# Quarter buffers for the weights of two experts, and a seventh buffer in the ring

## The chip, the core and the metric

The kernel runs on one core of a Trainium2 chip. The metric is the device time of one launch in microseconds (us); the numbers are fp32 throughout. TensorE (PE) does the matrix products, VectorE (DVE), ScalarE (ACT) and GpSimd (POOL) the rest, and SyncE (SP) issues the transfers (DMAs) that bring weights from the device's memory (HBM) into the core's on-chip memory of 128 partitions.

## The reference, cut to what matters

Two blocks of two layers each run over 256 tokens of width 1024. The first block is where the change lies: a gated linear recurrence and a mixture of experts, then a short convolution and a second mixture of experts. The second block is an S5 state space layer, a squared-ReLU MLP, latent attention and another MLP. A mixture of experts looks like this:

```python
def hierarchical_moe(h, w_group, b_group, w_expert, b_expert, w_gate, w_up, w_down):
    ...                                   # 4 groups of 8 experts, each token goes to 2 of 32
    def expert_block(args):
        xb, e = args
        hb = jax.nn.silu(xb @ w_gate[e]) * (xb @ w_up[e])     # 1024 -> 512
        return hb @ w_down[e]                                 # 512 -> 1024
    ...                                   # gated sum back into the tokens
```

An expert has three matrices of 2 MiB (gate, up, down). The kernel reads all 32 experts, so a mixture moves 192 MiB of weights.

## The kernel before, in words

`moe` (L771) handles the experts in eight groups of four; `e0` is the first expert of a group. A group's four experts are computed side by side: each has 32 token slots, and its products fill a band of 32 rows of PE's output. For one group the order of the program is: `load(e0)` asks for the weights (24 MiB), PE does the gate and up products (L963), ACT the SiLU (L971), DVE the product with up (L972), PE transposes (L977) and does the down products (L1002), ACT and DVE scale them into y (L1005, L1006), and PE adds y back to the tokens (L1014; DVE's addition is L1025). On every second group PE also gathers the tokens for the next two (L911, L912).

Weights come in through `fetch` (recorded as L447): it takes the next buffer of a ring and has SP issue a DMA of 1 MiB into it, 8 KB in each of the 128 partitions. SP waits, in order, until the last reader of the buffer's old contents is done; a buffer that isn't free stops every later load too. One buffer holds a half of one expert's matrix: four of its eight rows per partition (gate, up), one run of 8 KB. The loads of a group are gate half 0 of four experts, up half 0, gate half 1, up half 1, then eight for down. PE takes a block of 16 matmuls for gate or up in one half, four rows times four experts, in which the expert changes fastest. So a block needs four buffers, and all four are in use to its end.

The ring is long in layer two's mixture at first, 17 buffers, and is cut while group e0 = 8 runs: the generator `stages` (L1962), which the mixture advances at set points, calls `shrink` after 12 steps, and from then on the ring is the six buffers of the main pool. The space goes to `s5_prepare`, S5's tables, which the generator then works off in steps between the mixture's own instructions (E and cf on DVE, L1346 `pr`, L1380 and L1416 transposes on PE). A buffer more is added by `grow(1)` in `s5` (L1573) when S5's scan is over. The next loads after the mixture's own are S5's weights. A scheduler orders each engine's instructions by priority and dependence, so that a change of the loads also moves other instructions.

S5's scan keeps working arrays `ro0`, `ro1` and `hc` of 2 KB per partition each in a pool of its own.

Of the kernel before, what the change touches and what calls it, by code (L numbers as in the profile page):

```python
# [8 lines left out]
F32 = mybir.dt.float32  # L9
# [31 lines left out]
KV = 1  # L41
WARMB = 3
G3 = 5
EARLY = 1, 0
N0 = 4
FAST = (0, 1), (0, 1)
# [26 lines left out]
class Net:  # L73
# [697 lines left out]
    def moe(self, layer, rows, stages=()):  # L771


        nc, I, tc = self.nc, self.I, self.tc
# [7 lines left out]
        with ExitStack() as ph:  # L782
# [56 lines left out]
            def logits(n):  # L839
                v.tensor_tensor(lg[:, n, :], self.logits(layer, self.xt[n]), self.br[layer], op=OP.add)  # L840

            if EARLY[N == 3]:
                logits(0)
# [4 lines left out]
            for n in range(2):  # L848
                src = h[n].rearrange("t (p k) -> t k p", k=KD)
                self.pin(a.copy)(xh[n], src)  # L850
                nc.gpsimd.tensor_tensor(xl[n], src, xh[n].bitcast(F32), op=OP.subtract)
            if not EARLY[N == 3]:
                logits(0)
# [8 lines left out]
            for n in range(2):  # L862
                p = self.bank()
# [18 lines left out]
            def load(e):  # L882

                def half(w, hf):
                    out = []
                    for i in range(4):
                        src = w[layer, e + i].rearrange("(p k) f -> p k f", p=128)
                        k = src.shape[1] // 2
                        out.append(self.fetch(src[:, hf * k:hf * k + k, :], [128, k, src.shape[2]]))
                    return out  # L890

                gu = [[half(I[nm], hf) for nm in ("moe_w_gate", "moe_w_up")] for hf in range(2)]
                if e < 28:
                    return gu, [half(I["moe_w_down"], hf) for hf in range(2)]

                src = [I["moe_w_down"][layer, e + i].rearrange("(p k) f -> p k f", p=128) for i in range(4)]
                down = [[self.fetch(x[:, :, 0:512], [128, 4, 512]) for x in src], [self.fetch(None, [128, 4, 512]) for x in src]]
                for c in lasts[1:]:
                    for t, x in zip(down[1], src):
                        self.pin(nc.sync.dma_start)(t[:, :, c.start - 512:c.stop - 512], x[:, :, c])  # L900
                return gu, down
# [22 lines left out]
            def places(e0):  # L924
# [7 lines left out]
                return P  # L932

            first = load(0)
            P = places(0)
            xg_tile = lambda: B.tile([128, 4, 256], F32, name="xg", bufs=2)
            xg = [gather(xg_tile(), P, 256, 0)]
# [11 lines left out]
            for qd in range(8):  # L949

                e0, c0 = 4 * qd, 128 * (qd % 2)
                if qd % 2 == 0 and qd:
                    P, xg = places(e0), []
                wgu, wd = load(e0) if qd else first
                gu = [self.bank() for _ in range(2)]
                for hf in range(2):
                    if len(xg) == hf:
                        xg.append(gather(xg_tile(), P, 256, hf))
                    for m in range(2):
                        for k in range(4):  # L960
                            for i in range(4):
                                c = slice(c0 + 32 * i, c0 + 32 * i + 32)
                                nc.tensor.matmul(gu[m][i * 32:(i + 1) * 32, :], lhsT=xg[hf][:, k, c], rhs=wgu[hf][m][i][:, k, :],  # L963
                                                 start=hf == 0 and k == 0, stop=hf == 1 and k == 3)
                    if qd < 7:
                        next(stages, None)
                if N == 3 and qd == 0:
# [5 lines left out]
                if qd < 7:  # L973
                    next(stages, None)
                p = self.bank("tp")
# [6 lines left out]
                p = self.bank("tp")  # L982
# [15 lines left out]
                def down(c, j, w):  # L998

                    o = ob[c.start // 512][:, c.start % 512:(c.stop - 1) % 512 + 1]  # L1000
                    for e in range(4):
                        nc.tensor.matmul(o[e * 32:(e + 1) * 32, :], lhsT=ht[:, j, e * 32:(e + 1) * 32], rhs=w[e], start=j == 0, stop=j == 3)  # L1002
                    if j == 3:
                        yh, yl = (t[:, c.start % 512:(c.stop - 1) % 512 + 1] for t in y[c.start // 512])
                        a.activation(yh, o, AF.Copy, scale=gs)  # L1005
                        v.scalar_tensor_tensor(yl, o, gs, yh.bitcast(F32), op0=OP.mult, op1=OP.subtract)  # L1006
                        if N == 3 and qd < 7:
                            v.scalar_tensor_tensor(yo[:, c], o, gs, yo[:, c], op0=OP.mult, op1=OP.add)
# [8 lines left out]
                if qd < 7:  # L1017
                    for j in range(4):
                        for c in HALVES:
                            down(c, j, [wd[j // 2][e][:, j % 2, c] for e in range(4)])  # L1020
                        if j % 2:
                            next(stages, None)
                    for n in range(2):
                        for c in HALVES:
                            v.tensor_tensor(h[n][:, c], h[n][:, c], back(n, c), op=OP.add)  # L1025
                    next(stages, None)
                    continue
# [437 lines left out]
    def s5(self):  # L1465
        nc, I, h = self.nc, self.I, self.h
        v, a = nc.vector, nc.scalar
        BL, CL, KT, rho = self.BL, self.CL, self.KT, self.rho
        with ExitStack() as ph:
# [4 lines left out]
            keep = es.enter_context(self.pool("s5k"))  # L1474
# [9 lines left out]
            for q4 in range(4):  # L1484
                p = self.bank()
                for j in range(4):
                    for i, x in enumerate((xh, xl)):
                        nc.tensor.matmul(p, lhsT=self.place[:, 128 * q4 + 3 - j:128 * q4 + 131 - j], rhs=x[:, :, j:SEQ:4],  # L1488
                                         start=j + i == 0, stop=j + i == 4)
# [6 lines left out]
            B = es.enter_context(self.pool("s5b", 2))  # L1496

            ros, hcs = [], []
            for i in range(2):
                ros.append(keep.tile([128, 8, 64], F32, name=f"ro{i}"))  # L1500
                nc.gpsimd.memset(ros[i][:, :, 0:1], 0.0)
            for i in range(4):
                hcs.append([keep.tile([128, 8, 64], F32, name=f"hc{i}{n}") for n in range(2)])
                for n in range(2):
                    nc.gpsimd.memset(hcs[i][n][:, :, 0:1], 0.0)
            v8 = lambda ap: ap.rearrange("p (g n) -> p g n", g=8)
# [36 lines left out]
            for Q in range(4):  # L1543
                py = self.bank()
                for n in range(3):
                    for q in range(8):
                        for y in range(2):
# [5 lines left out]
                            else:  # L1553
                                l, r = hcs[(2 * Q + y) % 4][1][:, q, :], CS[:, g, :]
                            nc.tensor.matmul(py[y * 64:(y + 1) * 64, q * 64:(q + 1) * 64], lhsT=l, rhs=r,
                                             start=n + q == 0, stop=n == 2 and q == 7, skip_group_check=True)
# [6 lines left out]
                p = self.bank("tp")  # L1563
                for i in range(4):
                    nc.tensor.transpose(p[:, i * 128:(i + 1) * 128], yg[:, i].rearrange("p q c -> p (q c)"), self.ident)
                src = p.rearrange("p (i g n) -> p g i n", i=4, g=2)
                for g in range(2):
                    k = 2 * Q + g
# [1 line left out]
            es.close()  # L1570
            self.kept.close()
            self.wide = [(self.right.enter_context(self.pool(f"wide{n}", n, "right")), n) for n in (2, 3)]
            self.grow(1)  # L1573
            self.widen()
            self.F.append(self.ctx.enter_context(self.pool("fb")))
            S = ph.enter_context(self.pool("glus"))
# [375 lines left out]
    def stages0(self):  # L1952
# [4 lines left out]
        self.shrink()  # L1957
        self.grow(G3)
        self.wide_s = ExitStack()
        self.wide = self.wide_s.enter_context(self.pool("wide0", 3, "right"))  # L1960

    def stages(self):  # L1962

        for _ in range(NY):
            yield
        self.shrink()
        self.tables_now = False
        for _ in range(N0):
            yield
        yield from self.s5_prepare()  # L1970

    def run(self):
# [6 lines left out]
        self.wide_s.close()  # L1979
        self.grow(11 - G3)  # L1980
        self.moe(1, [128, 128], self.stages())
# [40 lines left out]
```

## Time and profile before

| what | value |
|---|---|
| median of 3 runs | 1988.52 us (1983.27 to 1994.42) |
| the profiled execution's own time | 1989.83 us |
| its span | 1988.1 us |
| mean granted TensorE clock | 0.906 of full speed |
| PE busy | 1630.0 us, 82% |
| DVE, ACT, POOL busy | 863.1, 508.0, 242.7 us |
| DMA queue of SP | 532.04 MB, 70.7% of 16 engines' span |
| gate/up matmuls, L963 | 410.5 us busy, 187.5 us idle before them |
| down matmuls, L1002 | 220.2 us busy, 17.7 us idle before them |

The span is the profiled execution from its first to its last instruction. A row of instructions gives what line, engine and operation it is, output and inputs by the program's names, and how many; "idle before" is the time in which the engine stood still just ahead of such instructions, with the one it waited for. A window row gives the busy time of each engine in a stretch of the span, the clock that TensorE was granted there as a share of its full speed, the share of time in which the 16 DMA engines were busy, and the traffic. The two rows of matmuls in the table take in both mixtures.

### The profile page before, as it was taken

To read this page: it belongs to the slowest core of one execution; us is meant where nothing else is said; L and a number is where in the kernel's file an instruction comes from. 1 tells how busy PE (TensorE), PEld (TensorE's weight loads), DVE (VectorE), ACT (ScalarE), POOL (GpSimd) and SP (SyncE) were. 2 spreads that over 40 slices of the span, in tenths; PEclk is the share of its full clock that TensorE was granted. 3 is DMA by queue.
4 is the path that set the end of the run, shared out by engine and by line. 5 is a ranking of instruction groups with operands and counts; after the bars stand their busy time and mean duration, and the time that the engine had idled before them with its cause. 6 is when DMAs were issued, how large, how long until landed. Compare 5 with 4: busy or idle time off the path is not lost.

```text
span 1988.1 us, 24934 instructions
## 1 busy us (share of the span) xinstructions
PE 1630.0 (82%) x10043; PEld 1014.4 (51%) x10044; DVE 863.1 (43%) x1724; ACT 508.0 (26%) x811; POOL 242.7 (12%) x263
## 2 busy tenths in 40 slices
PE   7878777777777978766768778678989998898997
PEld 6753211222126953212313222136979997878997
DVE  6872101111008661105313131176776556776555
ACT  4621000000004431000100100022545443564442
POOL 3330000000003230000000000015431003303000
PEclk9889989999898989987878879779899998999999
DMA  9358999999999657998786788884635542425540
GB/s 308 115 212 344 419 420 420 420 419 420 419 402 329 215 191 319 420 420 321 303 340 241 304 336 338 317 187 110 234 127 184 182 160 90 170 85 179 184 147 22
DMA packets 133113, 535.57 MB, mean 269 GB/s; under 512 B 23141, under 2 KB 35686, under 8 KB 85882
## 3 DMA queue, kind: packets, MB, share of 16 engines
q1 hardware_dynamic: 130818, 532.04, 70.7%
q0 software_dynamic: 1856, 1.75, 0.4%
q8 instruction: 81, 1.33, 0.3%
q14 instruction: 46, 0.38, 0.1%
q10 hardware_dynamic: 312, 0.07, 0.0%
HBM read 526.49 MB, written 1.05 MB: 265 GB/s over the span
## 4 chain that ended last, share of the span: by engine, by line
PE 37%; DMA 13%; DVE 7%; ACT 1%; issue 1%; POOL 1%; SPq 0%; DVEq 0%; POOLq 0%; ACTq 0%
DMA raw<-in_moe_w_gate 7%; PE mm L963 5%; PE mm L493 5%; PE mm L491 5%; PE mm L492 5%; DMA raw<-in_moe_w_up 4%; PE tp L492 3%; PE tp L493 3%; PE mm L1002 3%; PE tp L491 3%; DMA raw<-in_moe_w_down 2%; PE tp L1416 1%; DVE wlo L294 1%; PE mm L1488 1%; PE mm L1014 0%
## 5 line engine op out<-in xcount | busy, mean ns | idle before, releaser
L963 PE MATMUL mm<-raw,xg 128*32 128x512 f32 x2048 | 410.5, 738 | 187.5 <-DMA raw<-in_moe_w_up 113.7
L294 DVE TENSOR_TENSOR wlo<-raw,whi 128x1024 fp32r<-128x1024 f32 (+3 forms) x265 | 294.2, 1126 | 185.2 <-ACT whi L293 184.2
L963 PEld LDWEIGHTS mm<-raw,xg 128*32 128x32 f32 x2048 | 86.7, 130 | 494.9 <-DMA raw<-in_moe_w_up 193.5
L293 ACT CAST whi<-raw 128x1024 fp32r<-128x1024 f32 (+3 forms) x265 | 239.0, 917 | 252.7 <-PE mm L493 105.7
L972 DVE TENSOR_TENSOR hh<-hh,mm 128x512 f32<-128x512 f32 x16 | 11.0, 687 | 520.1 <-PE mm L963 520.1
L1002 PE MATMUL mm<-raw,ht 128*32 128x512 f32 (+2 forms) x1120 | 220.2, 612 | 17.7 <-DMA raw<-in_moe_w_down 14.2
L492 PE MATMUL tp<-f,whi 128*128 128x256 f32 x512 | 147.6, 288 | 11.5 <-DVE f L409 11.5
L493 PE MATMUL mm<-whi,f 128*128 128x512 f32 (+3 forms) x432 | 150.2, 348 | 2.1 <-DVE f L409 2.1
L491 PE MATMUL mm<-whi,f 128*128 128x512 f32 (+3 forms) x432 | 151.4, 350 | 0.0
L492 PE MATMUL mm<-wlo,f 128*128 128x512 f32 (+3 forms) x432 | 150.9, 349 | 0.0
L493 PE MATMUL tp<-f,wlo 128*128 128x256 f32 x512 | 146.9, 287 | 0.0
L491 PE MATMUL tp<-f,whi 128*128 128x256 f32 x512 | 146.6, 287 | 0.4 <-ACT f L403 0.2
L1002 PEld LDWEIGHTS mm<-raw,ht 128*32 128x32 f32 x1120 | 54.3, 118 | 142.9 <-issue 97.8
L971 ACT ACTIVATE hh<-mm 128x512 f32<-128x512 f32 x16 | 9.6, 597 | 430.3 <-PE mm L963 430.3
L492 PEld LDWEIGHTS tp<-f,whi 128*128 128x128 f32 x512 | 100.4, 196 | 12.0 <-POOL h L95 11.8
L491 PEld LDWEIGHTS tp<-f,whi 128*128 128x128 f32 x512 | 99.9, 196 | 1.2 <-ACT f L403 0.8
L493 PEld LDWEIGHTS tp<-f,wlo 128*128 128x128 f32 x512 | 100.5, 196 | 0.0
L492 PE MATMUL mm<-xl,whi 128*128 128x272 f32 (+2 forms) x320 | 93.9, 294 | 7.5 <-DVE xl L409 7.1
L491 PE MATMUL mm<-xh,whi 128*128 128x272 f32 (+2 forms) x320 | 93.1, 295 | 0.6 <-ACT yg L663 0.4
L493 PE MATMUL mm<-xh,wlo 128*128 128x272 f32 (+2 forms) x320 | 92.5, 290 | 0.0
L493 PEld LDWEIGHTS mm<-whi,f 128*128 128x128 f32 x432 | 82.3, 190 | 12.7 <-DVE f L409 2.7
L491 PEld LDWEIGHTS mm<-whi,f 128*128 128x128 f32 x432 | 82.6, 191 | 10.3
(609 smaller groups left out, 2504.9 us busy)
## 6 DMA issues: line engine op xcount, KB each, us to landing
raw<-in_moe_w_gate SPq DMA_DIRECT2D x128, 1024.0 KB, 10.3
raw<-in_moe_w_up SPq DMA_DIRECT2D x128, 1024.0 KB, 19.9
raw<-in_moe_w_down SPq DMA_DIRECT2D x120, 1024.0 KB, 16.8
raw<-in_w_ff SPq DMA_DIRECT2D x64, 1024.0 KB, 4.9
raw<-in_sc_w_in SPq DMA_DIRECT2D x12, 1024.0 KB, 12.4
raw<-in_lru_w_in SPq DMA_DIRECT2D x8, 1024.0 KB, 14.0
raw<-in_ssm_w_glu SPq DMA_DIRECT2D x8, 1024.0 KB, 10.7
raw<-in_moe_w_down SPq DMA_DIRECT2D x12, 512.0 KB, 13.3
```

The costliest lines, as they stand in the source:

```text
L293: f(self.nc.scalar.copy)(hi, src)
L294: f(self.nc.vector.tensor_tensor)(lo, src, hi.bitcast(F32), op=OP.subtract)
L491: mm(out, lhsT=lh, rhs=rh, start=first, stop=False, skip_group_check=shared)
L492: mm(out, lhsT=lh, rhs=rl, start=False, stop=False, skip_group_check=shared)
L493: mm(out, lhsT=ll, rhs=rh, start=False, stop=last, skip_group_check=shared)
L963: nc.tensor.matmul(gu[m][i * 32:(i + 1) * 32, :], lhsT=xg[hf][:, k, c], rhs=wgu[hf][m][i][:, k, :], start=hf == 0 and k == 0, stop=hf == 1 ...
L971: a.activation(hh, gu[0], AF.Silu)
L972: v.tensor_tensor(hh, hh, gu[1], op=OP.mult)
L1002: nc.tensor.matmul(o[e * 32:(e + 1) * 32, :], lhsT=ht[:, j, e * 32:(e + 1) * 32], rhs=w[e], start=j == 0, stop=j == 3)
L1416: nc.tensor.matmul(po[:, :, j:4, :], lhsT=sel[:, 67 - 64 * g - j:195 - 64 * g - j], rhs=Kg[:, g, :, 0:4 - j, :], start=n == 0, stop=n == 7)
L1488: nc.tensor.matmul(p, lhsT=self.place[:, 128 * q4 + 3 - j:128 * q4 + 131 - j], rhs=x[:, :, j:SEQ:4], start=j + i == 0, stop=j + i == 4)
```

## The change

A constant FINE = 8 selects layer two's groups from e0 = 8 on. There `load` no longer fills a buffer with half a matrix of one expert but with a quarter of two: two of eight rows for gate and up (one of four for down) of the experts i and i + 1, each in a run of 4 KB per partition, the two experts' matrices lying 2 MiB apart in HBM. Gate and up alternate by quarters, so loads come in pairs. The matmuls of a half are cut into parts of two rows accordingly, 8 matmuls for gate, 8 for up. Down loads in the groups up to e0 = 24 are quarters too; the last group's keep their shape. Directly behind `shrink` a `grow(1)` makes the ring seven buffers long, and the one in `s5` is gone. S5's scan takes `ro0`, `ro1` and the two arrays `hc` of index 0 from one ring buffer.

```diff
@@ -41,6 +41,7 @@
 KV = 1
 WARMB = 3
 G3 = 5
+FINE = 8
 EARLY = 1, 0
 N0 = 4
 FAST = (0, 1), (0, 1)
@@ -889,9 +890,23 @@
                         out.append(self.fetch(src[:, hf * k:hf * k + k, :], [128, k, src.shape[2]]))
                     return out
 
-                gu = [[half(I[nm], hf) for nm in ("moe_w_gate", "moe_w_up")] for hf in range(2)]
+                def quarter(w, kq):
+
+                    out = []
+                    for i in (0, 2):
+                        src = w[layer, e + i:e + i + 2].rearrange("e (p k) f -> p e k f", p=128)
+                        k = src.shape[2] // 4
+                        t = self.fetch(src[:, :, kq * k:kq * k + k, :], [128, 2, k, src.shape[3]])
+                        out += [t[:, 0], t[:, 1]]
+                    return out
+
+                fine = layer == 1 and e >= FINE
+                if fine:
+                    gu = [[quarter(I[nm], kq) for nm in ("moe_w_gate", "moe_w_up")] for kq in range(4)]
+                else:
+                    gu = [[half(I[nm], hf) for nm in ("moe_w_gate", "moe_w_up")] for hf in range(2)]
                 if e < 28:
-                    return gu, [half(I["moe_w_down"], hf) for hf in range(2)]
+                    return gu, [quarter(I["moe_w_down"], j) for j in range(4)] if fine else [half(I["moe_w_down"], hf) for hf in range(2)]
 
                 src = [I["moe_w_down"][layer, e + i].rearrange("(p k) f -> p k f", p=128) for i in range(4)]
                 down = [[self.fetch(x[:, :, 0:512], [128, 4, 512]) for x in src], [self.fetch(None, [128, 4, 512]) for x in src]]
@@ -956,12 +971,15 @@
                 for hf in range(2):
                     if len(xg) == hf:
                         xg.append(gather(xg_tile(), P, 256, hf))
-                    for m in range(2):
-                        for k in range(4):
-                            for i in range(4):
-                                c = slice(c0 + 32 * i, c0 + 32 * i + 32)
-                                nc.tensor.matmul(gu[m][i * 32:(i + 1) * 32, :], lhsT=xg[hf][:, k, c], rhs=wgu[hf][m][i][:, k, :],
-                                                 start=hf == 0 and k == 0, stop=hf == 1 and k == 3)
+
+                    n = len(wgu) // 2
+                    for part in range(n):
+                        for m in range(2):
+                            for k in range(4 // n * part, 4 // n * (part + 1)):
+                                for i in range(4):
+                                    c = slice(c0 + 32 * i, c0 + 32 * i + 32)
+                                    nc.tensor.matmul(gu[m][i * 32:(i + 1) * 32, :], lhsT=xg[hf][:, k, c], rhs=wgu[hf * n + part][m][i][:, k % (4 // n), :],
+                                                     start=hf == 0 and k == 0, stop=hf == 1 and k == 3)
                     if qd < 7:
                         next(stages, None)
                 if N == 3 and qd == 0:
@@ -1017,7 +1035,8 @@
                 if qd < 7:
                     for j in range(4):
                         for c in HALVES:
-                            down(c, j, [wd[j // 2][e][:, j % 2, c] for e in range(4)])
+                            k = 4 // len(wd)
+                            down(c, j, [wd[j // k][e][:, j % k, c] for e in range(4)])
                         if j % 2:
                             next(stages, None)
                     for n in range(2):
@@ -1496,11 +1515,12 @@
             B = es.enter_context(self.pool("s5b", 2))
 
             ros, hcs = [], []
+            t = self.fetch(None, [128, 4, 8, 64])
             for i in range(2):
-                ros.append(keep.tile([128, 8, 64], F32, name=f"ro{i}"))
+                ros.append(t[:, i])
                 nc.gpsimd.memset(ros[i][:, :, 0:1], 0.0)
             for i in range(4):
-                hcs.append([keep.tile([128, 8, 64], F32, name=f"hc{i}{n}") for n in range(2)])
+                hcs.append([keep.tile([128, 8, 64], F32, name=f"hc{i}{n}") if i else t[:, 2 + n] for n in range(2)])
                 for n in range(2):
                     nc.gpsimd.memset(hcs[i][n][:, :, 0:1], 0.0)
             v8 = lambda ap: ap.rearrange("p (g n) -> p g n", g=8)
@@ -1570,7 +1590,6 @@
             es.close()
             self.kept.close()
             self.wide = [(self.right.enter_context(self.pool(f"wide{n}", n, "right")), n) for n in (2, 3)]
-            self.grow(1)
             self.widen()
             self.F.append(self.ctx.enter_context(self.pool("fb")))
             S = ph.enter_context(self.pool("glus"))
@@ -1964,6 +1983,7 @@
         for _ in range(NY):
             yield
         self.shrink()
+        self.grow(1)
         self.tables_now = False
         for _ in range(N0):
             yield
```

On SP the loads of group e0 = 12 read before:

```order
L447 DMA raw<-in_moe_w_gate 128x2048 x4
L447 DMA raw<-in_moe_w_up 128x2048 x4
L447 DMA raw<-in_moe_w_gate 128x2048 x4
L447 DMA raw<-in_moe_w_up 128x2048 x4
L447 DMA raw<-in_moe_w_down 128x2048 x8
```

and now (the line of `fetch` is L448 there):

```order
L448 DMA raw<-in_moe_w_gate 128x2x1024 x2
L448 DMA raw<-in_moe_w_up 128x2x1024 x2
L448 DMA raw<-in_moe_w_gate 128x2x1024 x2
L448 DMA raw<-in_moe_w_up 128x2x1024 x2
L448 DMA raw<-in_moe_w_gate 128x2x1024 x2
L448 DMA raw<-in_moe_w_up 128x2x1024 x2
L448 DMA raw<-in_moe_w_gate 128x2x1024 x2
L448 DMA raw<-in_moe_w_up 128x2x1024 x2
L448 DMA raw<-in_moe_w_down 128x2x1024 x8
```

The count is the same, 16 and 8; gate and up change after every pair instead of every fourth load.

On PE the beginning of the down products of group e0 = 12 reads before as follows (`ht` is the transposed hidden activation, W a table of S5, xh and xl the tokens that are gathered for the next groups):

```order
L1002 MATMUL mm<-raw,ht 32x512 x4
L1380 MATMUL tp<-ident,W 128x128 x8
L911 MATMUL tp<-P_7283,xh_5360 128x256
L912 MATMUL tp<-P_7283,xl_5362 128x256
L911 MATMUL tp<-P_7285,xh_5361 128x256
L912 MATMUL tp<-P_7285,xl_5363 128x256
```

and now, in lines L1020, L1399, L926 and L927:

```order
L1399 MATMUL tp<-ident,W 128x128 x2
L1020 MATMUL mm<-raw,ht 32x512 x4
L1399 MATMUL tp<-ident,W 128x128 x6
L926 MATMUL tp<-P_7286,xh_5360 128x256
L927 MATMUL tp<-P_7286,xl_5362 128x256
L926 MATMUL tp<-P_7288,xh_5361 128x256
L927 MATMUL tp<-P_7288,xl_5363 128x256
L1020 MATMUL mm<-raw,ht 32x512 x4
```

The down products stand in fours, with one gather's four matmuls between the first and the second four; before, fifteen gather matmuls stood there.

On DVE the scaling y of group e0 = 8 and the exponential of S5's preparation (E, mg) read before:

```order
L1201 SCALAR_TENSOR_TENSOR E<-E 128x64
L1006 SCALAR_TENSOR_TENSOR y_6807<-mm,gs,y_6806 128x512
L261 SCALAR_TENSOR_TENSOR E<-E 128x64
L1238 CAST place<-ident 128x128
L1006 SCALAR_TENSOR_TENSOR y_6809<-mm,gs,y_6808 128x512
```

and now, where y is L1024:

```order
L262 SCALAR_TENSOR_TENSOR E<-E 128x64 x3
L263 TENSOR_SCALAR E<-E 128x64
L265 TENSOR_TENSOR mg<-E 128x64
L1298 TENSOR_TENSOR p_7034<-mg,w_6906 128x64
L1024 SCALAR_TENSOR_TENSOR y_6810<-mm,gs,y_6809 128x512
L1024 SCALAR_TENSOR_TENSOR y_6812<-mm,gs,y_6811 128x512
```

The rest of the exponential, up to the first product with mg, has moved ahead of y.

## Rows read from the trace of the kernel before

**Rows 1.** The page, part 2: GB/s that the DMA engines moved, in 40 slices.

```profile
...
GB/s 308 115 212 344 419 420 420 420 419 420 419 402 329 215 191 319 420 420 321 303 340 241 304 336 338 317 187 110 234 127 184 182 160 90 170 85 179 184 147 22
...
```

**Rows 2.** Windows of layer two's MoE; columns: us, busy, PEclk, DMA share, GB/s.

```profile
912.60:957.00 44.40, 29.53 (x129) 6.01 (x128) 17.53 (x72) 1.76 (x4) 0.00 (x0) 0.73 0.83 323
957.00:994.90 37.90, 30.60 (x198) 14.96 (x202) 18.48 (x37) 8.11 (x14) 0.98 (x2) 0.90 0.77 297
994.90:1037.20 42.30, 27.88 (x128) 5.60 (x128) 3.74 (x6) 0.60 (x1) 0.00 (x0) 0.73 0.84 333
1037.20:1081.20 44.00, 41.70 (x190) 18.55 (x190) 8.08 (x17) 3.13 (x5) 0.00 (x0) 0.81 0.56 217
1081.20:1125.90 44.70, 29.38 (x133) 6.09 (x132) 11.41 (x21) 1.85 (x3) 0.00 (x0) 0.77 0.87 350
1125.90:1162.20 36.30, 28.87 (x197) 14.68 (x197) 17.68 (x35) 8.12 (x14) 0.00 (x0) 0.94 0.80 316
1162.20:1206.10 43.90, 29.50 (x129) 5.79 (x128) 3.80 (x6) 0.60 (x1) 0.00 (x0) 0.74 0.80 315
1206.10:1233.50 27.40, 26.09 (x162) 12.07 (x162) 7.78 (x17) 2.54 (x4) 0.00 (x0) 1.00 0.84 329
1233.50:1281.50 48.00, 29.35 (x129) 5.68 (x128) 1.78 (x3) 0.60 (x1) 0.00 (x0) 0.79 0.85 336
1281.50:1317.00 35.50, 26.61 (x170) 13.93 (x170) 28.44 (x95) 3.07 (x6) 0.21 (x2) 0.68 0.71 206
```

**Rows 3.** Chain of waits, 907 to 1000 us; columns: start us, us, what.

```profile
...
912.62 4.00 PE mm L963 x31
916.62 8.12 DMA raw<-in_moe_w_up
924.78 5.28 PE mm L963 x27
930.07 7.08 DMA raw<-in_moe_w_gate
...
942.99 7.38 DMA raw<-in_moe_w_up
950.41 6.52 PE mm L963 x26
...
```

**Rows 4.** Waits, 912.6 to 1281.5 us; columns: total us, times, longest us.

```profile
...
PE mm L963 <- DMA raw<-in_moe_w_up: 49.8, 23, 4.5
...
PE mm L963 <- DMA raw<-in_moe_w_gate: 27.6, 14, 4.0
...
```

**Rows 5.** Waits of SP's DMA queue, 907 to 1282 us.

```profile
...
SPq L447 <- PE mm L963: 209.2, 29, 11.5
...
```

**Rows 6.** Timeline of SP's DMA issues, 905 to 960 us.

```profile
...
908.76 8.24 SPq L447 DMA_DIRECT2D raw<-in_moe_w_up  x4
917.10 13.35 SPq L447 DMA_DIRECT2D raw<-in_moe_w_gate  x4
930.54 12.82 SPq L447 DMA_DIRECT2D raw<-in_moe_w_up  x4
943.76 14.05 SPq L447 DMA_DIRECT2D raw<-in_moe_w_down  x6
```

**Rows 7.** DMA view of four windows in turn: 200:230, 642.5:648.5, 608:626, 1300:1304.

```profile
DMA packets 1732, 12.61 MB, mean 420 GB/s; under 512 B 194, under 2 KB 194, under 8 KB 194
...
DMA packets 641, 2.49 MB, mean 416 GB/s; under 512 B 32, under 2 KB 32, under 8 KB 641
...
DMA packets 3501, 6.96 MB, mean 387 GB/s; under 512 B 107, under 2 KB 107, under 8 KB 3500
...
DMA packets 2228, 1.12 MB, mean 281 GB/s; under 512 B 66, under 2 KB 2228, under 8 KB 2228
...
```

**Rows 8.** Timeline of DVE, 908 to 930 us.

```profile
...
914.23 0.22 DVE L261 SCALAR_TENSOR_TENSOR E<-E 128x64 f32<-128x64 f32 x1
...
916.09 0.36 DVE L1279 TENSOR_TENSOR p<-mg,w 128x64 f32<-128x64 f32 x2
...
```

## The prediction, made before the changed kernel ran

> **What bounds the kernel now.** I read the page's traffic line first [rows 1]: one slice is 49.7 us, and where only weights of the mixtures of experts move it stands flat at 420 GB/s (slices 8 to 11, layer one), while in slices 19 to 26, the second half of layer two's mixture, it stands at 241 to 340. The work per expert is the same, so something holds the loads back there. The windows of that stretch, cut at the first and last gate/up matmul of each group of four experts, come next [rows 2]: the rows alternate, a gate/up stretch (44.4, 42.3, 44.7, 43.9 and 48.0 us for the groups e0 = 12, 16, 20, 24, 28) and then what lies between (down products, routing, preparation of S5). In each gate/up stretch PE is busy some 29 us of 44 at a granted clock of 0.73 to 0.79, and DMA 0.80 to 0.87: neither is full, so they take turns. The chain of waits says how [rows 3]: a block of 16 matmuls (4.00 us), a wait of 8.12 us that ends with the landing of "up", a block of 5.28, a wait of 7.08, and so on. A block needs four buffers and frees the four together at its end. The ring has six here, so two loads run beside the block, and the other two are issued only when it ends: 2 x 2.50 us of transfer (1 MiB at 420 GB/s [rows 7]) and 2.1 to 3.1 us more before the bytes flow. SP's timeline shows the same from its side [rows 6]: it issues four loads, then waits, and the bursts start 13.4 and 13.2 us apart (917.10, 930.54, 943.76) where four transfers take 10.0. PE's waits for gate and up in the five stretches sum to 49.8 + 27.6 = 77.4 us [rows 4], and SP's wait for gate/up matmuls to free buffers is 209.2 us [rows 5].
>
> **The change: the loads.** Two quarter buffers now hold two of a matrix's eight rows per partition for all four experts, where four half buffers held four rows. So a block is 8 matmuls, needs two buffers and frees two. Bytes, count of loads (16 and 8 per group) and matmuls are the same. With seven buffers, two are read and five are on order: 5 x 2.5 = 12.6 us of transfer ordered ahead of a block of 2.0 to 3.3 us (half of the 4.00 to 6.52 in [rows 3]). The DMA does not run dry between blocks, and a gate/up stretch then lasts as long as its missing loads take.
>
> The price of one load: a partition's run shrinks from 8 KB to 4 KB. The trace has saturated windows of both [rows 7]: 420 GB/s with 8 KB packets (12.61 MB in 1732 packets) and 416 with 4 KB (2.49 MB in 641), so 2.50 and 2.52 us for 1 MiB. Two experts' runs lie 2 MiB apart in one load, which no row shows. Bounds: nothing, and from the other side the rate of 281 GB/s of the worst cut in the trace (half-KB packets), 3.73 us. I take 2.52, since the nearest row in packet size is the 416 one.
>
> Now the five stretches, each counted as loads still missing at its first matmul:
> - e0 = 16, 20, 24: the stretch before must bring 8 down loads and 7 of the next gate/up, 15 x 2.52 = 37.8 us. Those stretches last 37.9, 44.0 and 36.3 us [rows 2], so the ring is full, or within one load of it, when the first block starts. Left are 9 loads: first block 2.0, 2.6 until bytes flow again (the middle of 2.1 to 3.1), 9 x 2.52 = 22.7, last block 2.0: 29.3 us.
> - e0 = 12: the ring has just been cut from 17 buffers; the first block's data is there at 912.6 and the next loads are ordered at 908.76 [rows 6]. 12 loads are missing: 908.76 + 2.6 + 12 x 2.52 + 2.0 = 943.6, so 31.0 us.
> - e0 = 28: the stretch before is 27.4 us, which is 10.9 loads, 8 of them down: 3 in hand, 13 missing: 32.8 + 2.0 = 34.8 us, and the DMA never stopped.
>
> Savings: 44.4 - 31.0 = 13.4; 42.3 - 29.3 = 13.0; 44.7 - 29.3 = 15.4; 43.9 - 29.3 = 14.6; 48.0 - 34.8 = 13.2. Sum 69.6 us. PE doesn't limit: four blocks of the slowest kind in [rows 3], 6.52 us, are 26.1, still under 29.3. If it ran so through all five stretches the cover would be 3 us each.
>
> **The change: what it moves.** Down loads come in pairs too (e0 = 12 to 24; the last group's keep their shape), and PE's down matmuls go in fours, each behind its own pair, with S5's transposes and the next gather between them. The first pair is ordered right behind the last gate/up pair and lands 2 x 2.52 = 5.0 us after it. PE reaches it after a block of 2.0 and an estimated 2 us of SiLU, product and transposes (in the trace the four buffers of the old first down block were on order from 943.76 on, long before [rows 6]). That is a wait of about 1 us in four stretches, and the gather and the S5 transposes queue behind it on PE: +4. Bounds: 0 (other work is scheduled ahead of it) and 5.0 each, +20, if nothing is.
> DVE's y of group 8 now stands behind the whole exponential of S5's preparation: what passed it are the rows from 914.23 to 916.09 [rows 8], about 2 us. PE's first gate/up block of group 12 waits for it in PE's order, but the loads of that group are what ends it and they are issued before. I take 0; without that cover it is +2.
> Four of S5's working arrays sit in a ring slot now, and the growth of the ring moves from behind S5 to the shrink. Memory set and copies into the slot wait for down products long finished, and SP issues the loads of S5's weights behind them as before: 0, bounds -1 to +3. The tail from 1281.5 on has DVE busy 28.44 of 35.5 us [rows 2], on tables that don't change: 0, down to -1.
>
> Sum: 69.6 - 4 = 65.6 us less, from the profiled execution's own 1989.83 (span 1988.1): 1924.2. That execution lies 1.3 us above the median of the runs, so I say 1923.
>
> **A rule that speaks against it.** No row shows one load whose two runs per partition lie 2 MiB apart. The Trainium skill ("DMA: Bandwidth & Descriptors", section "Latency and other measured facts") lists copies whose partitions lie a large power of two apart: at 2 MiB it states 164 GB/s, where the full rate in that test was 214. Here partitions stay 16 KB apart and only the two runs of one partition jump; if the rule held all the same, an estimate from that page would be 2.52 x 214 / 164 = 3.3 us a load, which comes out some 13 us slower than before. By itself it is a part of the slower rival below.
>
> **The rivals.**
> - *The wait moves to the stretches between.* The full ring holds next gate/up buffers, so nothing more is issued until PE is back, and down pairs arrive late with S5's chain and the gather queued behind. Price: two loads and a restart, 5.0 + 2.6 = 7.6 us, in four stretches: 30 us of the gain lost, 1954. For: PE is busy 41.70 of 44.0 in the longest of these stretches, and 26.09 of 27.4 in the shortest [rows 2], so no slack takes up a delay. Against: eight down loads take 20.2 us, less than any of these stretches.
> - *The change doesn't do what it says*: buffers of a pair still come free with four, and only the seventh counts. It spares one load of 2.5 us in each of three waits of five stretches: 38 us, 1952. Against: the program's order on SP has pairs.
> - *Slower: the split loads are slow.* Place: the DMA engines from 907 us on, through 108 loads (5 x 24 gate/up and down, less 8 down of the last group and 4 already there). The forecast has the last gate/up end at 1211; that is 907 + 108 x 2.52 and 32 us of pauses. With r us for a load it ends at 939 + 108 r, against 1281.5 before: it decides from r = 3.17 us (331 GB/s). At 3.73 it ends at 1342, 60 us later than before: 2050. For: two runs per partition in different experts are shown nowhere. Against: 4, 2 and half-KB packets cost 2.52, 2.71 and 3.73, and this cut is the first of them; at the 2.71 of the 387 GB/s row, 20 of the gain goes, 1944.
> - *More*: the stalls also held the clock at 0.73 to 0.79 where the shortest stretch between has 1.00 [rows 2]. If the stretches between at 0.81 to 0.94 also came to 1.00, their PE time of 30.60, 41.70 and 28.87 would shrink by 3.1, 7.9 and 1.7 us: 12.7 more, 1911.
>
> **How the numbers follow.** About 0.5%, 10 us, is what a measurement of this kernel can tell from none. Forecast 0.68, with a range of its own of 1908 to 1940 (up to the 16 us that the down wait's far end adds, down to no down wait and most of the clock's 12.7). The wait moves 0.13; only the seventh buffer 0.05; slow loads 0.06, half of it at a rate near 2.7 with some gain left; more than 1908 holds 0.08. The range of 8 in 10: 1904 to 1948. Faster by over 0.5%: all but the slow half and accidents, 0.95; same 0.02; slower 0.03.
>
> **What would show it.** Right: in the gate/up windows DMA at about 1.0 and 410 GB/s, lengths of 29 to 35 us, SP's issues in twos some 5 us apart, PE's waits there short but as many as blocks. Load wrong: windows full at a lower GB/s. Down wrong: stretches between longer than 38, 44, 36 and 27 us with PE waiting for down. The seventh buffer alone: issues still in fours. The forecast is wrong if the last gate/up ends later than 1230 us into the span, or if S5 and what follows it, from 1317 on, is longer than before.

## The result, and the profile after

The changed kernel takes 1924.66 us (median of 4 runs, 1921.11 to 1929.49) against 1989.16 us before (4 runs, 1983.27 to 1994.42): ratio 0.9674, 95% interval 0.9656 to 0.9692. The forecast was 1923. The profiled span fell from 1988.1 to 1924.2 us, 63.9 us. What lies ahead of the gate/up products of the group e0 = 12 and behind the last group's barely moved: that stretch starts at 912.5 and 912.6 us, and what follows it lasted 706.6 us (1281.5 to 1988.1) and lasts 708.1 (1216.1 to 1924.2).

Here are the windows of the changed kernel, cut at the first and last gate/up matmul of the groups e0 = 12 to 28 as in [rows 2], and the whole stretch in the last row. Columns: us, busy time of PE, PEld, DVE, ACT, POOL (instructions), granted clock, DMA share, GB/s.

```profile
...
912.60:949.40 36.80, 22.46 (x129) 4.17 (x128) 15.60 (x61) 1.28 (x2) 0.00 (x0) 1.00 1.03 409
949.40:982.70 33.30, 26.91 (x200) 13.82 (x202) 18.61 (x37) 8.12 (x14) 0.98 (x2) 0.92 1.03 399
982.70:1016.20 33.50, 23.69 (x129) 4.54 (x128) 3.50 (x6) 0.60 (x1) 0.00 (x0) 0.86 1.00 395
1016.20:1056.10 39.90, 37.70 (x194) 18.43 (x194) 7.85 (x17) 3.72 (x6) 0.00 (x0) 0.84 0.91 327
1056.10:1087.40 31.30, 21.40 (x129) 4.26 (x128) 11.84 (x21) 1.26 (x2) 0.00 (x0) 0.95 0.93 362
1087.40:1120.70 33.30, 26.88 (x198) 13.80 (x196) 17.80 (x35) 8.12 (x14) 0.00 (x0) 0.95 1.03 409
1120.70:1153.40 32.70, 23.35 (x129) 4.68 (x128) 3.54 (x6) 0.60 (x1) 0.00 (x0) 0.84 0.91 359
1153.40:1180.10 26.70, 24.03 (x162) 12.16 (x162) 7.87 (x17) 2.54 (x4) 0.00 (x0) 1.00 1.03 409
1180.10:1216.10 36.00, 25.46 (x129) 4.99 (x128) 1.77 (x3) 0.60 (x1) 0.00 (x0) 0.86 1.03 406
912.60:1216.10 303.50, 231.89 (x1385) 80.87 (x1384) 88.37 (x199) 26.83 (x45) 0.98 (x2) 0.91 0.99 385
...
```

The same whole stretch before:

```profile
...
912.50:1281.50 369.00, 272.99 (x1385) 89.49 (x1384) 90.38 (x210) 27.31 (x47) 0.98 (x2) 0.81 0.80 313
...
```

The DMA's share over the stretch rose from 0.80 to 0.99, the granted clock from 0.81 to 0.91. A full window reads 1.02 or 1.03 in this view, not 1.00. The share rose in both kinds of stretch: gate/up from 0.80-0.87 to 0.91-1.03, between from 0.56-0.84 to 0.91-1.03. The gate/up stretches sum to 170.3 us (223.3 in [rows 2]), those between to 133.2 (145.6). The granted clock in the gate/up rows is 0.84 to 1.00, where it was 0.73 to 0.79. The page's traffic line, against [rows 1]:

```profile
...
GB/s 307 130 219 296 420 419 421 419 420 420 420 420 378 235 169 210 419 413 387 409 393 327 391 375 409 253 169 111 260 117 190 192 142 90 161 112 161 195 132 22
...
```

SP's issues, the counterpart of [rows 6], come in pairs, 5.1 us apart.

```profile
...
918.75 4.66 SPq L448 DMA_DIRECT2D raw<-in_moe_w_up  x2
923.88 4.65 SPq L448 DMA_DIRECT2D raw<-in_moe_w_gate  x2
928.99 4.67 SPq L448 DMA_DIRECT2D raw<-in_moe_w_up  x2
934.11 20.28 SPq L448 DMA_DIRECT2D raw<-in_moe_w_down  x8
...
```

Of the chain of waits, the counterpart of [rows 3], the pieces of the group e0 = 12:

```profile
...
894.31 22.45 DMA raw<-in_moe_w_up
...
916.80 1.11 PE mm L981 x8
917.93 14.18 DMA raw<-in_moe_w_gate
932.16 1.11 PE mm L981 x8
933.28 14.18 DMA raw<-in_moe_w_up
...
947.50 1.94 PE mm L981 x12
...
```

In this group the chain no longer alternates a block with the landing of loads issued at its end. It is a row of landings 14 to 22 us long: loads queued behind each other on a DMA that doesn't stop, with pieces of 1.1 us on PE between. PE's waits for gate and up are 53.7 us in place of 77.4 [rows 4]:

```profile
...
PE mm L981 <- DMA raw<-in_moe_w_up: 32.0, 27, 2.8
...
PE mm L981 <- DMA raw<-in_moe_w_gate: 21.7, 20, 2.6
...
```

And a row that stood beside that of [rows 5] and that the prediction did not use: SP's waits for down products to free buffers, before and after. Columns: total us, times, longest us.

```profile
...
SPq L447 <- PE mm L1002: 109.8, 12, 22.5
...
```

```profile
...
SPq L448 <- PE mm L1020: 87.0, 29, 6.8
...
```

The longest such wait fell from 22.5 to 6.8 us.

### The profile page after: what moved, and what is told of

Same layout as the page of the kernel before. It is cut to its first block, busy times and chain, and to the rows that moved or that the text cites. A ratio compares the mean times of both kernels' runs of the same rounds, so it can differ in the third digit from the quotient of the medians.

```text
span 1924.2 us, 24928 instructions
## 1 busy us (share of the span) xinstructions
PE 1589.4 (83%) x10036; PEld 1007.2 (52%) x10044; DVE 863.3 (45%) x1724; ACT 507.5 (26%) x811; POOL 243.0 (13%) x263
## 4 chain that ended last, share of the span: by engine, by line
PE 36%; DMA 14%; DVE 7%; ACT 1%; issue 1%; POOL 1%; SPq 0%; DVEq 0%; ACTq 0%; POOLq 0%
DMA raw<-in_moe_w_up 9%; PE mm L494 5%; PE mm L492 5%; PE mm L493 5%; PE tp L493 3%; PE tp L494 3%; PE tp L492 3%; DMA raw<-in_moe_w_gate 3%; PE mm L981 3%; PE mm L1020 3%; DMA raw<-in_moe_w_down 2%; PE tp L1435 1%; PE mm L1507 1%; DVE wlo L295 1%; PE mm L1032 1%
## 5 line engine op out<-in xcount | busy, mean ns | idle before, releaser
L981 PE MATMUL mm<-raw,xg 128*32 128x512 f32 x2048 | 381.3, 687 | 164.9 <-DMA raw<-in_moe_w_up 97.5
L981 PEld LDWEIGHTS mm<-raw,xg 128*32 128x32 f32 x2048 | 80.5, 120 | 448.7 <-DMA raw<-in_moe_w_up 173.4
L1020 PE MATMUL mm<-raw,ht 128*32 128x512 f32 (+2 forms) x1120 | 208.5, 610 | 15.7 <-DMA raw<-in_moe_w_down 11.9
L1020 PEld LDWEIGHTS mm<-raw,ht 128*32 128x32 f32 x1120 | 53.0, 118 | 128.4 <-issue 86.8
```

## The experiments

The ratios below are each to runs of the kernel before on the same chip. Stretch means first gate/up matmul of e0 = 12 to the last of e0 = 28; its windows give DMA share and GB/s. A profile is one execution: its own time stands beside the median, and "from" is where its stretch begins. The beginnings lie between 906 and 917 us, why is not shown; what follows the stretch lasts 706 to 711 us in all of them.

| kernel | gate/up | down | ring | median us | ratio (95%) | profiled us | from us | gate/up sum | between sum | share | GB/s |
|---|---|---|---|---|---|---|---|---|---|---|---|
| before | halves | halves | 6 | 1989.16 | 1 | 1989.83 | 912.5 | 223.3 | 145.6 | 0.80 | 313 |
| e8 | halves | quarters | 6 | 1965.98 | 0.9882 (0.9856-0.9908) | 1966.27 | 912.5 | 221.5 | 124.2 | 0.85 | 334 |
| e1 | halves | halves | 7 | 1955.19 | 0.9832 (0.9806-0.9857) | 1955.96 | 911.5 | 190.3 | 143.8 | 0.86 | 345 |
| e6 | quarters | halves | 7 | 1950.37 | 0.9809 (0.9783-0.9835) | 1947.02 | 914.7 | 175.0 | 149.1 | 0.90 | 358 |
| e2 | quarters | quarters | 6 | 1943.05 | 0.9760 (0.9738-0.9781) | 1947.74 | 916.7 | 175.8 | 142.5 | 0.93 | 360 |
| e7 | halves | quarters | 7 | 1926.33 | 0.9706 (0.9660-0.9753) | 1918.43 | 906.1 | 185.9 | 118.0 | 0.97 | 387 |
| the change | quarters | quarters | 7 | 1924.66 | 0.9674 (0.9656-0.9692) | 1925.98 | 912.6 | 170.3 | 133.2 | 0.99 | 385 |

**e1, the seventh buffer alone.**

```diff
-FINE = 8
+FINE = 32
```

> Half buffers of one expert as before, seven buffers in the ring. Theory A (blocks that free four buffers at once leave the DMA dry; the cut into pairs is what counts): three loads instead of two run beside a block, so each of 15 waits loses one load of 2.5 us, 38 us at the most: about 1952, the issues still in fours, DMA share in the gate/up stretches about 0.9. Rival B (the ring's depth is what counts): about 1925, as with the whole change.

1955.19 us: the forecast's rival price (1952) and theory A's. Two of its windows between and the whole stretch:

```profile
...
949.90:987.80 37.90, 30.52 (x199) 14.91 (x199) 18.45 (x37) 8.11 (x14) 0.98 (x2) 0.89 0.80 306
1024.80:1067.20 42.40, 40.06 (x191) 18.32 (x191) 8.15 (x17) 3.13 (x5) 0.00 (x0) 0.84 0.61 234
911.50:1245.60 334.10, 254.50 (x1385) 88.39 (x1384) 90.47 (x210) 27.29 (x47) 0.98 (x2) 0.86 0.86 345
...
```

The gate/up stretches got 33 us shorter, but between them the DMA still stands at 0.80 and 0.61, near the 0.77 and 0.56 of [rows 2].

**e2, the quarters alone** (`grow(1)` behind S5 again, its arrays in their own pool).

> Quarter buffers of two experts, six buffers in the ring, S5's arrays and the ring's growth as before. Theory A: four loads ahead of a block of 8 matmuls still keep the DMA busy in the gate/up stretches; one load less in hand at the start of a stretch costs up to 2.6 us where the ring is full, in three or four stretches: 1926 to 1936. Rival B (depth): about 1988.

1943.05 us, 7 above theory A's range and far from B's. Both parts count; neither alone is the gain.

```profile
...
916.70:1235.00 318.30, 241.69 (x1385) 83.09 (x1384) 88.24 (x199) 26.79 (x45) 0.98 (x2) 0.89 0.93 360
...
```

**e6, down stays in halves.**

```diff
-return gu, [quarter(I["moe_w_down"], j) for j in range(4)] if fine else [half(...) for hf in range(2)]
+return gu, [half(I["moe_w_down"], hf) for hf in range(2)]
```

> As the change, but down loads stay halves of one expert; PE's down products stand in pieces of two matmuls again. Theory A, with the DMA as the bound from 912 to 1217 us: the stretches between get some 4 us longer each, but the loads run on meanwhile and the gate/up stretches get shorter by as much: 1922 to 1930. Rival C (the 14.6 us that the stretches between lost are a gain of their own, from down products that stand in fours on PE): 1925 + 14.6 = about 1939.

1950.37 us: both theories missed. All five gate/up stretches are full (share 1.02 or 1.03), most of the loss is between (149.1 us in place of 133.2):

```profile
...
950.70:986.60 35.90, 28.62 (x198) 15.07 (x199) 19.93 (x39) 8.13 (x14) 0.98 (x2) 0.93 0.88 341
1018.80:1060.30 41.50, 38.83 (x194) 17.98 (x194) 10.54 (x21) 3.72 (x6) 0.00 (x0) 0.88 0.65 257
914.70:1238.80 324.10, 251.00 (x1385) 86.83 (x1384) 90.01 (x210) 27.37 (x47) 0.98 (x2) 0.88 0.90 358
...
```

**e7, only down in quarters.**

```diff
-                if fine:
+                if False:
                     gu = [[quarter(...
```

> Gate and up as half buffers, down as quarters of two experts, seven buffers. Theory A: blocks of gate and up free four at once again, so about as with the seventh buffer alone, 1952, less what the pieces of four on PE give where the DMA isn't the bound. Rival C: 14.6 us less than with the seventh buffer alone, about 1937.

1926.33 us, by its interval not to be told from the whole change. Theory A as I held it falls: with seven buffers and the down cut, the cut of gate and up, which the prediction put first, is worth nothing that these runs can tell (four runs from 1918 to 1941 us; the profile is of the fastest). A small gain isn't excluded: the three pairs with seven buffers that differ in it alone (e1 and e6, e7 and the change, e14 and e15) all lean its way, by 0.002 to 0.004 of the time, each within its intervals. The stretches between are full now; of those of gate and up, the third (0.83, last but one row) and the fourth (0.89) are not:

```profile
...
947.70:977.70 30.00, 24.23 (x196) 13.09 (x196) 17.94 (x36) 8.13 (x14) 0.98 (x2) 0.98 1.02 402
1012.20:1045.00 32.80, 30.45 (x176) 14.27 (x176) 7.87 (x17) 2.55 (x4) 0.00 (x0) 0.95 1.02 408
1045.00:1084.40 39.40, 27.13 (x147) 7.63 (x146) 11.66 (x21) 2.42 (x4) 0.00 (x0) 0.83 0.83 324
906.10:1210.00 303.90, 226.02 (x1385) 81.72 (x1384) 88.58 (x199) 26.84 (x45) 0.98 (x2) 0.91 0.97 387
...
```

**e8, the down cut with six buffers** (e7 and e2's edits together). From here on theory D: the DMA's standing still anywhere in the stretch sets the end.

> Gate and up halves, down quarters of two experts, six buffers, S5's arrays as before: the down cut by itself. The first four kernels gave 1955 (halves, seven buffers), 1950 (gate and up cut), 1926 (down cut), 1925 (both, the change). Theory D: the DMA's idle time sets the end, in the stretches between as in those of gate and up, and there it is the down buffers, held by four through PE's other work, that stop it. Then the down cut gives its 29 us with six buffers too: about 1961. Rival A (gate/up blocks that free four are the bound): within 5 us of before, 1985 to 1991.

1965.98 us, a gain of 22 by the down cut alone. In the gate/up stretches the DMA idles much as before (0.72 to 0.89); of those between three are full (1.00 or 1.01), the second stands at 0.82. The first of each kind, and the whole stretch:

```profile
...
912.50:957.30 44.80, 30.22 (x129) 5.93 (x128) 15.78 (x61) 1.25 (x2) 0.00 (x0) 0.73 0.83 324
957.30:987.80 30.50, 24.71 (x198) 13.51 (x198) 18.05 (x36) 8.11 (x14) 0.98 (x2) 0.94 1.01 391
912.50:1258.20 345.70, 257.35 (x1385) 87.16 (x1384) 88.67 (x199) 26.76 (x45) 0.98 (x2) 0.80 0.85 334
...
```

With six buffers the cut of gate and up is worth 23 us on top (e2 against e8, intervals apart); with seven it can't be told from none (the change against e7).

**e10, twelve loads less.**

```diff
-gu = [[quarter(I[nm], kq) for nm in ("moe_w_gate", "moe_w_up")] for kq in range(4)]
+gu = [[quarter(I[nm], kq) for nm in ("moe_w_gate", "moe_w_up")] for kq in range(3)]
+gu.append([quarter(I["moe_w_gate"], 3), gu[2][1]])
```

> As the change, but the last quarter of up isn't loaded in the groups from e0 = 8 on; PE takes the buffers of the third quarter again. 12 loads of 1 MiB less, the same instructions on the engines. Theory D: 12 x 2.56 = 31 us less, about 1894. If PE or the order of the releases is the bound: at most 5 us less, 1920.

1896.35 us (ratio 0.9544, 0.9528 to 0.9561): 28 us less than the change (26 by the ratios), where 12 loads at 2.56 are 31. The engines' instructions are the same, so the changed kernel is bound by its loads here. Ten of the twelve lie in the stretch, which is 22.9 us shorter than the change's; two belong to the group e0 = 8 ahead of it, and it begins 7.9 us earlier.

```profile
...
904.70:1185.30 280.60, 221.20 (x1395) 81.86 (x1394) 93.41 (x230) 27.20 (x47) 2.33 (x5) 0.91 0.98 382
...
```

**e3, one expert a load.**

```diff
-t = self.fetch(src[:, :, kq * k:kq * k + k, :], [128, 2, k, src.shape[3]])
+t = self.fetch(None, [128, 2, k, src.shape[3]])
+for x in range(2):
+    nc.sync.dma_start(t[:, x], src[:, x, kq * k:kq * k + k, :])
```

> As the change, but each quarter buffer is filled by two loads of 512 KB, one for each expert: the same 4 KB runs, no load that spans two experts. The program's order has PE's down products in twos again here. If two runs 2 MiB apart are what took the rate from 416 to 409 GB/s, the 110 loads get 0.04 us shorter: about 1920. If not, and the order of the down products doesn't count where the DMA is the bound (theory D): 1923 to 1930. Rival C (fours on PE are the gain): 1925 + 14 = 1939.

1938.44 us. The rate answers the question it was made for: a full window has 409 GB/s, what the change has in its full windows, so the jump of 2 MiB within a load costs nothing that shows. The time is rival C's number, but not only through the down products: PE is busy 278.04 us in the stretch, 231.89 in the change, and in the gate/up row it is nearly bound by itself (29.91 of 34.4 us). Of the stretch's 18.6 us more than in the change, 15.1 lie between.

```profile
...
983.90:1018.30 34.40, 29.91 (x131) 5.92 (x130) 2.21 (x4) 0.60 (x1) 0.00 (x0) 0.95 0.85 332
1167.60:1196.30 28.70, 26.21 (x166) 12.77 (x169) 7.85 (x17) 2.44 (x4) 0.00 (x0) 0.94 1.03 409
907.30:1229.40 322.10, 278.04 (x1385) 88.02 (x1384) 88.40 (x198) 26.50 (x45) 0.98 (x2) 0.94 0.94 363
...
```

**e5, runs of 2 KB.**

```diff
+def eighth(w, kq):
+    src = w[layer, e:e + 4].rearrange("e (p k) f -> p e k f", p=128)
+    t = self.fetch(src[:, :, kq:kq + 1, :], [128, 4, 1, src.shape[3]])
+    return [t[:, i] for i in range(4)]
...
-gu = [[quarter(I[nm], kq) for nm in ("moe_w_gate", "moe_w_up")] for kq in range(4)]
+gu = [[eighth(I[nm], kq) for nm in ("moe_w_gate", "moe_w_up")] for kq in range(8)]
```

> As the change, but a gate or up buffer holds one of eight rows of four experts, in runs of 2 KB; PE frees one buffer after every four matmuls. Theory D with the rate of the trace's 2 KB packets, 387 GB/s or 2.71 us a load: 96 such loads, 0.15 us each, 14 us slower than the change: about 1939. If finer releases still help more than the shorter runs cost: 1925 or less.

1950.36 us (ratio 0.9819, 0.9802 to 0.9836), slower than the change by more than expected. The DMA is full; the stretch is 13.8 us longer than the change's, near the 14 of the estimate, and begins 2.2 us later (the group e0 = 8 ahead of it is cut alike). In the profiled execution, the fastest of its four, that is nearly all: its span, 1941.8, is 17.6 above the change's. The other 8 us of the median's 26 I can't place.

```profile
...
990.30:1022.50 32.20, 22.57 (x129) 3.46 (x128) 3.57 (x6) 0.60 (x1) 0.00 (x0) 0.66 1.03 383
914.80:1232.10 317.30, 247.75 (x1385) 80.90 (x1384) 88.43 (x199) 26.83 (x45) 0.98 (x2) 0.72 0.99 368
...
```

**e11, rival C by itself.** Was it that the down products stood in fours on PE? In the kernel before, a piece of two matmuls takes as long as a piece of four (each matmul is two records, and the granted clock is 1.00 at both):

```profile
...
959.19 1.92 PE L1002 MATMUL mm<-raw,ht 128*32 128x512 f32 x8
...
964.35 1.90 PE L1002 MATMUL mm<-raw,ht 128*32 128x512 f32 x4
...
```

Taking the experts in reverse order lets the first matmul wait for the buffer that lands last, and the four stand together without any change of the buffers.

```diff
-for e in range(4):
+for e in range(4) if layer == 0 or e0 < 8 else (3, 2, 1, 0):
     nc.tensor.matmul(o[e * 32:(e + 1) * 32, :], lhsT=ht[:, j, e * 32:(e + 1) * 32], rhs=w[e], ...
```

> As the seventh buffer alone (half buffers, 1955), but PE takes the four experts of a down product in the order 3, 2, 1, 0 in layer two from e0 = 8 on, so that the first waits for the last buffer and the four stand together; the program's order shows down products in runs of 16 in place of pieces of 2, 10 and 12. Buffers still come free four at a time. Theory D (the down cut gains by releasing in pairs while PE is at other work): PE's down products get 12 us shorter in all, as they did in the change (220.2 to 208.5), at most that shows: 1943 to 1955. Rival C (pieces of four side by side on PE are what the down cut gains): about 1926.

1951.07 us (ratio 0.9801, 0.9775 to 0.9827). PE's time for down products fell by 21 us, from the first row (e1) to the second (e11); columns: busy us (when several run side by side, the time counts once), mean ns of one, idle before.

```profile
...
L1020 PE MATMUL mm<-raw,ht 128*32 128x512 f32 x256 | 66.8, 684 | 0.5 <-ACT ht L997 0.2
...
```

```profile
...
L1020 PE MATMUL mm<-raw,ht 128*32 128x512 f32 x264 | 46.0, 850 | 8.5 <-DMA raw<-in_moe_w_down 8.5
...
```

The kernel gained 4 us by the medians and 6 by the ratios, with intervals that overlap. None of it lies in the stretch, which is as long as in e1 (334.4 and 334.1 us) and begins 5.9 us earlier. PE now waits 8.5 us for down loads to land, and the DMA still stands between:

```profile
...
946.70:982.20 35.50, 26.18 (x196) 15.46 (x195) 20.58 (x40) 8.32 (x14) 0.98 (x2) 0.76 0.79 300
1020.60:1057.50 36.90, 32.84 (x195) 18.99 (x195) 12.46 (x24) 4.15 (x7) 0.00 (x0) 0.77 0.62 239
905.60:1240.00 334.40, 242.02 (x1388) 91.53 (x1387) 93.61 (x223) 28.07 (x48) 1.97 (x4) 0.82 0.88 350
...
```

Rival C falls as the whole cause: e7 lies another 19 us lower by the ratios (0.9706 and 0.9801, intervals apart).

**e12, e14, e15: the same order on e6, e7 and the change.**

> As the change with half buffers for down (1950), with the same reversed order. Theory D: 1938 to 1950. Rival C: about 1925.

> As the down cut with seven buffers (1926), with the same reversed order; runs of 8 to 24 in place of 4 to 12. Both theories: the DMA is near its limit (0.97 of the stretch from 906 to 1210), so 1918 to 1927; Rival C puts it at the lower end.

> As the change (1925), with the same reversed order. The DMA stood at 0.99 there: no more than 5 us to gain, 1919 to 1926, by either theory.

e12: 1945.98 us (ratio 0.9764, 0.9739 to 0.9790), as theory D had it. Its stretch is 328.7 us, e6's 324.1, though PE is busy with down products 32 us less in it (41.6 after 73.4). e14: 1934.18 (0.9704, 0.9666 to 0.9741), above the range in us, but the ratio is e7's. e15: 1922.20 (0.9664, 0.9642 to 0.9685), the lowest of the kernels with all loads, though not to be told from the change (0.9656 to 0.9692). Its DMA share over the stretch is 1.00, in its fastest execution (1913.84):

```profile
...
906.80:1205.40 298.60, 216.03 (x1385) 80.04 (x1384) 88.75 (x202) 27.05 (x45) 0.98 (x2) 0.87 1.00 392
...
```

So the order on PE by itself shortens nothing in the stretch while halves come free by four (e11, e12). Whether the release by pairs would do it by itself, with down products in twos, is not shown: e3 is nearest to it, and its stretch is 322.1 us after e6's 324.1, but PE's gate and up products take longer there as well (busy 150.9 us in the five gate/up stretches, 122.6 in e6). What is shown is that the down cut, which brings both, fills the DMA between and gains (e7, e8).

## Why the prediction came out, and where it failed

The number was right, the mechanism half so: that the DMA runs dry because buffers come free four at a time and too few are on order. The place was half wrong: it ran dry between the gate/up stretches as well.

- **The savings in the gate/up stretches, 69.6 us, failed as a size.** They were 53.0 (223.3 to 170.3): 36.8, 33.5, 31.3, 32.7 and 36.0 us measured, 31.0, 29.3, 29.3, 29.3 and 34.8 forecast. For e0 = 12 I counted the first block's four loads as there; the second of its up loads landed at 916.76 (894.31 + 22.45 in the chain), 4 us into the stretch, the queue ahead of it being full. From there 12 loads at 2.56 us and the last piece of 1.94 give 949.4, the measured end. For e0 = 16 the ring wasn't full: the stretch before was 33.3 us and not 37.9, which at its 399 GB/s is 12.7 loads and not 15. Reckoned alike, the next three had 12.4, 13.0 and 10.4, where I had 15, 15 and 10.9.
- **The stretches between, +4 us, failed in sign.** They lost 12.4. PE's wait for down loads, which the +4 stood for, doesn't show: no such row is among PE's waits in the stretch. Of the 12.4, PE's down products in fours account for 9.7: in the four stretches they keep PE busy 16.57, 21.88, 14.88 and 15.43 us before and 13.18, 19.59, 13.18 and 13.17 after. I described that order and gave it no price.
- **The loads between had no source.** I took the stretches between as PE's own, from PE busy 26 to 42 us in them, and assumed in the sum that 15 loads come in during them, without asking what lets them. Before, the DMA stood at 0.56 to 0.84 there [rows 2]; the rows were on my page. Down halves come free by four, with PE's S5 and gather work between the products that read them: SP's longest wait for them is 22.5 us, in e1 as well (row below), and 6.8 in the change. That it is this hold that stopped the DMA fits e7 and e8, but the cut that ends it also puts the products in fours.
- **The two errors cancelled**: 53.0 + 12.4 - 1.5 behind the stretch = 63.9, where I had 65.6. In part they had to, since with the DMA at 0.99 the end is set by the sum of the loads (e10); that they met within 2 us is luck. Length times DMA share of the stretch is 295 us before and in e7, 294 in e8, 287 in e1, 292 in e6, 296 in e2, 300 in the change: nearly the same work for the DMA each time, so what differs is mostly the time in which it stands still. The count in the rival of the slow loads is the better sum: 907 + 108 loads at the measured 2.56 leave 32.6 us up to 1216.1, where it had 32. (Its own end, 1211, leaves out the +4; by the forecast's sum it is 1215.9.) By the traffic, 385 GB/s against 409 in full windows, some 18 of the 32.6 are pauses of the DMA; the rest isn't placed.
- **Price of a load**: 2.52 us forecast, 2.56 measured (409 GB/s in full windows). The Trainium skill's row on large power-of-two pitches ("DMA: Bandwidth & Descriptors", "Latency and other measured facts"), from which the estimate was 3.3 us a load, doesn't bear on two runs of one partition 2 MiB apart: 409 GB/s with the jump, 409 without it in a full window of e3.
- **The rivals.** The seventh buffer alone was priced at 1952 and takes 1955.19; the change is more than that, by the down cut above all. The wait that moves to the stretches between didn't come. Slow loads didn't come. Of the clock's gain, part came: 0.91 over the stretch after 0.81, but PE wasn't what ended it.
- DVE's y behind the exponential cost nothing that shows, since the first gate/up matmul of e0 = 12 starts at 912.60, as before.

The row of e1, as SP waits for down products:

```profile
...
SPq L448 <- PE mm L1020: 121.2, 14, 22.5
...
```

Open: how much of the down cut's gain is the release by pairs and how much the fours on PE, given that the fours alone gain nothing; how much of e3's 13 us is PE's pieces and how much the doubled number of loads; e5's last 8 us; why the stretch begins at 905 us in one kernel and at 917 in another.

## What to carry to other kernels

When a ring of buffers feeds an engine, look up the DMA's share in every stretch, also where the engine is busy and waits for nothing: buffers that are held through other work can stop the loads there, and the bill comes at the next block. If the loads are the bound, the time in which the DMA stands still is what counts, and each cure (a buffer more, a finer release here or there) is worth what the others leave of it, so price them together and not one by one. A new cut of the buffers can also change what stands side by side on the engine; test the two apart before you say which of them gained.

## What the hardware showed

A piece of two fp32 matmuls of 32 columns takes the time of four side by side (1.90 and 1.92 us, 5 us apart in one stretch, the granted clock 1.00 at both). Loads in runs of 4 KB are steady at 409 GB/s over windows of 11 to 15 MB, and in runs of 2 KB at 387 (e5, 1003 to 1015 us), as in the trace before, which had 420 with runs of 8 KB and 416 with 4 KB in a window of 6 us [rows 7]. With the finest cut (e5) PE's granted clock over the stretch was 0.72, the lowest of all kernels here, with the DMA at 0.99.
